# Entry of a feed-forward network: ScalarE's steps put one product behind VectorE's, the chain of operands reordered, weight sums formed ahead of the low parts

## The chip, the cores and the metric

One Trainium2 chip, one core. The time is device microseconds (us) of one execution of the whole program. The kernel before takes 2473.96 us, the median of 3 runs (2471.93 to 2474.3).

## What is computed

One inference step of a one-layer streaming encoder over 544 tokens (512 prompt frames and 32 frames of a running stream), model width 2048, feed-forward width 5632, all in float32. Cut to what the change touches:

```python
mix, s_new, lat_new, kr_new = token_mixer(h, ...)      # ends with  ... @ w_out
h = layer_norm(ALPHA * h + mix, ln1_g, ln1_b)
ff, conv_new = conv_ffn(h, ...)

def conv_ffn(x, conv_buf, w_up, w_gate, conv_w, conv_b, w_down):
    u = x @ w_up
    ext = jnp.concatenate([conv_buf, u], axis=1)
    a = conv_b + sum(ext[:, j:j + T] * conv_w[j] for j in range(CONV_W))
    h = jax.nn.silu(a) * (x @ w_gate)
    return h @ w_down, ext[:, -(CONV_W - 1):]
```

## The kernel before, in words

Activations lie transposed: features on the 128 partitions, tokens along the free axis, in two token halves of 272 (`j` = 0 and 1). Every float32 product is made of three fp32r products, high by high, high by low and low by high. So each operand x is split: `high` (ScalarE, ACT) writes the rounded x, `low` (VectorE, DVE) writes x minus the rounded x. Weights are split in the same way: 512 KB of raw weights land in a `raw` slot, ACT writes `wh` (`rounded`, L962, or `split_w`, L104), DVE writes `wl` (L963, L105). Three `wh` and three `wl` buffers go round.

**The entry.** The layer norm's input z stands in `za` (blocks 0 to 7, feature half 1) and `zb` (blocks 8 to 15, feature half 2). The output projection finishes token half 0 first. Its statistics (sums over partitions by TensorE, L816; means and scales spread back by TensorE, L821) are taken while TensorE (PE) does the last three column groups of token half 1, twelve steps of 24 matmuls (`step`, list `TASKS`). During these, z of token half 0 is normalised in groups of four blocks, `G0` and `G1`: `centred` (DVE, L1119) subtracts the mean, `scaled` (DVE, L1122) multiplies, `affine` (ACT, L1127, four activations and, from ACT's own queue, a DMA that saves the result), then `high` (ACT, L1084) and `low` (DVE, L1088). The weights of the next step are split in between (`split_next`).

**The products.** The up and gate projections use Strassen's seven products (Winograd's form) on 2 by 2 blocks: feature half by token half. The operands are "11" and "12" (token half 0), "21" and "22" (token half 1), and the sums s1, s2, s4, s3 built from them (`summed`, L1473). The weights need sums too: `form` (DVE, L955, in place in a raw slot) and then `prep` (split into wh and wl). One entry of the list `items` is one product with one of the two weight matrices, 24 matmuls of 272 columns (L1011). Pairs of blocks 0 and 1 start as plain products of token half 0, which need only "11" and "12"; product 13 of the list is the first that reads "21", products 21 to 28 read s1, s2, s4, s3 in that order, two of each.

**What sets the order.** The order on PE, DVE and ACT is written out by hand (`manual_schedule`): each engine runs its instructions in the order in which the code issues them. `play` goes through `items`; at each it issues the product, then `prep` of the product two ahead, then `form` of the product three ahead. After that it spends what room is left on `need`, a list that makes the operands of token half 1 step by step (`chain`), each step charged 1.3 us of DVE time; `flush` runs steps early where the next product reads an operand that isn't done. Each step of `chain` names DVE and ACT instructions together. The loads of raw weights are issued by SyncE (SP) as slots come free (`pump`).

The statistics of token half 1 are taken between the first two products of the feed-forward network: `items[0].multiply()`, then `finish(6, ...)` adds the last column group into z and into the sums, then PE's sums of `stats`, then `items[1].multiply()`.

Of the kernel before, what the change touches and what calls it, by code (L numbers as in the profile page):

```python
# [57 lines left out]
def tile_encoder_step(ctx, tc, xp, xs, w_in, w_kr, w_q_b, w_kv_b, w_out, w_up, w_gate, w_down, w_down2,  # L58
# [87 lines left out]
    def pair_half(ps, j):  # L146
        n = H_[j].stop - H_[j].start
        return [ps[:, 512 * t:512 * t + n] for t in range(2)]

    def run(*gens):  # L150
        for g in gens:
            for _ in g:
                pass
# [636 lines left out]
    def acc_tile():  # L790
        seq[0] += 1
        if seq[0] % 2:
            return main_tile()
        return psA.tile([P, 1024], F32, name="acc", tag="acc")

    class Norm:
# [97 lines left out]
        def scale(self, z, e1, e2):  # L894
            z = z[:, self.cols]
            e1.tensor_tensor(out=z, in0=z, in1=self.mub, op=ALU.subtract)
            e2.tensor_tensor(out=z, in0=z, in1=self.rsb, op=ALU.mult)
            return z
# [34 lines left out]
    free, pending, fills, need, gated, retired = [], [], [], [], set(), set()  # L933
# [7 lines left out]
    def pump():  # L941
        while pending and free:
            g, key, src, n = pending.pop(0)
            p, tag = free.pop(0)
            t = p.tile([P, n * P], F32, name=tag, tag=tag)
            dma(t, src)
            g.raw[key] = Raw((p, tag), t)
# [132 lines left out]

    apx = ctx.enter_context(ExitStack())

    def high(name, src, ks):
        A.activation(x1_op[name][ks.start // GK][:, 0], src, AF.Copy)  # L1084

    def low(name, src, ks):
        t = x1_op[name][ks.start // GK]
        V.tensor_tensor(out=t[:, 1], in0=src, in1=t[:, 0].bitcast(F32), op=ALU.subtract)  # L1088

# [25 lines left out]
    def block(b, ks, j):  # L1115
        return (za, zb)[b][:, ks, H_[j]]

    def centred(b, ks, j):
        V.tensor_tensor(out=block(b, ks, j), in0=block(b, ks, j), in1=wide(nrm[j].mub), op=ALU.subtract)  # L1119

    def scaled(b, ks, j):
        V.tensor_tensor(out=block(b, ks, j), in0=block(b, ks, j), in1=wide(nrm[j].rsb), op=ALU.mult)  # L1122

    def affine(b, ks, j):
        for k in range(ks.start, ks.stop):
            zk = zt[b * HK + k][:, H_[j]]
            A.activation(zk, zk, AF.Identity, bias=col(C_LN1_B + b * HK + k), scale=col(C_LN1_G + b * HK + k))  # L1127
        A.dma_start(x1_dr[b][:, ks, H_[j]], block(b, ks, j))

    for t in range(2):  # L1130
        for j in range(2):
            z = zt[t][:, H_[j]]
# [180 lines left out]
    def chunk_of(p):  # L1313
        for g, n in enumerate(CHUNKS):
            if p < n:
                return g, p
            p -= n

    def flush(names):
        while need and any(n not in done for n in names):  # L1320
            need.pop(0)()
            late_need[0] -= 1.3

    done = {"11", "12"}

    def play(items, n0, hooks):

        for n in range(n0, len(items)):
            it = items[n]
            room = it.time  # L1330
            if n and items[n - 1].sink:
                room -= items[n - 1].sink()
            flush((it.name,))
            it.multiply()
            if n + 2 < len(items) and not hasattr(items[n + 2], "w"):
                room -= items[n + 2].prep()
            if n + 3 < len(items):
                pump()
                room -= items[n + 3].form()
            for f in hooks.get(n, ()):  # L1340
                f()
            if need and started:
                late_need[0] += room
                while need and late_need[0] > 0.6:
                    need.pop(0)()
                    late_need[0] -= 1.3
            else:
                drain(room)
            pump()
        items[-1].sink()  # L1350

    late_need, started = [0.0], set()

    with tc.manual_schedule():

# [31 lines left out]
        G0, G1 = GROUPS  # L1387
# [5 lines left out]
        def first_split():  # L1393
# [7 lines left out]
        first_w = []  # L1401
        x11, x12 = (lambda ks, b=b: block(b, ks, 0) for b in range(2))
        halves = [pair_half(acc_tile(), 1) for _ in range(3)]
        TASKS = [
            [lambda: next(stats0), lambda: next(stats0), lambda: [shifted(k, 1) for k in (14, 15, 10)]],
            [lambda: next(stats0), lambda: run(stats0), split_next, lambda: [shifted(k, 1) for k in (11, 12, 13)]],
            [split_next, lambda: centred(0, G0, 0), lambda: scaled(0, G0, 0)],
            [split_next, lambda: centred(0, G1, 0), lambda: affine(0, G0, 0), lambda: scaled(0, G1, 0)],
            [split_next, lambda: finish(7, halves[0]), lambda: affine(0, G1, 0)],
            [split_next, lambda: centred(1, G0, 0), lambda: high("11", x11(G0), G0), lambda: scaled(1, G0, 0)],  # L1410
            [split_next, lambda: high("11", x11(G1), G1), lambda: low("11", x11(G0), G0)],
            [split_next, lambda: affine(1, G0, 0), lambda: low("11", x11(G1), G1)],
            [split_next, lambda: finish(5, halves[1])],
            [first_split],
            [lambda: centred(1, G1, 0), lambda: scaled(1, G1, 0), lambda: affine(1, G1, 0)],
            [lambda: high("12", x12(G0), G0), lambda: high("12", x12(G1), G1)],
        ]
        for n, tasks in enumerate(TASKS):
            step(halves[n // 4], ws7[n] if n < 4 else ws[n - 4], 1, n % 4)
# [4 lines left out]
        items = p0.plain(0, e0)  # L1424
# [14 lines left out]
        finish(6, halves[2])  # L1439
        st_ps = main_tile()  # L1440
        stats = nrm[1].stats(ps=st_ps)
        next(stats)
        next(stats)
        low("12", x12(G0), G0)
        items[1].multiply()
        for it, t in zip(items[2:], sr):
            it.w = rounded(t, HK)
        next(stats)
        run(stats)
        low("12", x12(G1), G1)  # L1450
        st_stack.close()
        ff = ctx.enter_context(pool("ff"))
        ea = ff.tile([P, 4, 546], F32, name="ea", tag="ea")
# [18 lines left out]
        def summed(out, a, b, ks, f):  # L1472
            V.tensor_tensor(out=out[:, ks], in0=a[:, ks], in1=b[:, ks], op=f)  # L1473
# [9 lines left out]
        def open_late():  # L1483
# [3 lines left out]
            add_slots(lt, "rawl", 2)  # L1487

        ADD, SUB = ALU.add, ALU.subtract
        chain = [  # L1490
            [lambda: centred(0, G0, 1)],
            [lambda: scaled(0, G0, 1)],
            [lambda: affine(0, G0, 1), lambda: centred(0, G1, 1)],
            [lambda: scaled(0, G1, 1)],
            [lambda: high("21", a21[:, G0], G0), lambda: affine(0, G1, 1), lambda: centred(1, G0, 1)],
            [lambda: low("21", a21[:, G0], G0)],
            [lambda: scaled(1, G0, 1), lambda: high("21", a21[:, G1], G1)],
            [lambda: affine(1, G0, 1), lambda: centred(1, G1, 1)],
            [lambda: low("21", a21[:, G1], G1), lambda: done.add("21")],
            [lambda: scaled(1, G1, 1), lambda: high("22", a22[:, G0], G0), lambda: affine(1, G1, 1)],  # L1500
            [lambda: low("22", a22[:, G0], G0), lambda: high("22", a22[:, G1], G1)],
            [lambda: summed(a22, a21, a22, G0, ADD)],
            [lambda: low("22", a22[:, G1], G1), lambda: done.add("22"), lambda: high("s1", a22[:, G0], G0)],
            [lambda: summed(a22, a21, a22, G1, ADD)],
            [lambda: low("s1", a22[:, G0], G0), lambda: high("s1", a22[:, G1], G1)],
            [lambda: summed(a22, a22, a11, G0, SUB)],
            [lambda: low("s1", a22[:, G1], G1), lambda: done.add("s1"), lambda: high("s2", a22[:, G0], G0)],
            [lambda: summed(a22, a22, a11, G1, SUB)],
            [lambda: low("s2", a22[:, G0], G0), lambda: high("s2", a22[:, G1], G1)],
            [lambda: summed(a12, a12, a22, G0, SUB), close_wo],  # L1510
            [lambda: low("s2", a22[:, G1], G1), lambda: done.add("s2"), lambda: high("s4", a12[:, G0], G0)],
            [lambda: summed(a12, a12, a22, G1, SUB)],
            [lambda: low("s4", a12[:, G0], G0), lambda: high("s4", a12[:, G1], G1)],
            [lambda: summed(a21, a11, a21, G0, SUB)],
            [lambda: low("s4", a12[:, G1], G1), lambda: done.add("s4"), close_zb, lambda: high("s3", a21[:, G0], G0)],
            [lambda: summed(a21, a11, a21, G1, SUB)],
            [lambda: low("s3", a21[:, G0], G0), lambda: high("s3", a21[:, G1], G1)],
            [lambda: low("s3", a21[:, G1], G1), lambda: done.add("s3"), open_late],
        ]
        need += [lambda fs=fs: [f() for f in fs] for fs in chain]  # L1520


        ysq = [None] * 4
# [44 lines left out]
        class Whole:  # L1568

            n, name = 8, "11"  # L1570
# [28 lines left out]
        NU = len(items)  # L1599
# [11 lines left out]
        def at(n, f):  # L1611
            hooks.setdefault(n, []).append(f)
# [13 lines left out]
        def split_group(g, i):  # L1626
            for b, name in enumerate(("11", "12")):
                t = home[name].tile([P, 2, 2, T], R, name=f"hid{name}", tag=f"op{name}{i}")
                for f in range(2):
                    split_hid(FD + 4 * g + 2 * b + f, staged[g][:, 2 * b + f], t[:, f, 0], t[:, f, 1])  # L1630

        at(2, lambda: started.add(1))
        at(16, late12)
        for i, name in enumerate(ORDER):
# [378 lines left out]
```

## Time and profile before

| | us |
|---|---|
| median of 3 runs | 2473.96 |
| the profiled execution's own time | 2472.49 |
| its span in the profile | 2470.7 |
| PE busy in the span | 2400.2 (97%) |
| DVE busy | 1661.2 (67%) |
| ACT busy | 981.3 (40%) |
| mean granted clock of TensorE, as a share of full | 0.988 |

The profile is of one execution. A busy PE is one with matmuls in flight. The granted clock of TensorE is 1.00 (2.4 GHz) or 0.50 (1.2 GHz); values between are means over a stretch that holds both. In the timeline the bracket at the end of a row says how long the engine had stood idle before it and which instruction ended that.

### The profile page before, as it was taken

To read this page: it belongs to the slowest core of one execution; us is meant where nothing else is said; L and a number is where in the kernel's file an instruction comes from. 1 tells how busy PE (TensorE), PEld (TensorE's weight loads), DVE (VectorE), ACT (ScalarE), POOL (GpSimd) and SP (SyncE) were. 2 spreads that over 40 slices of the span, in tenths; PEclk is the share of its full clock that TensorE was granted. 3 is DMA by queue.
4 is the path that set the end of the run, shared out by engine and by line. 5 is a ranking of instruction groups with operands and counts; after the bars stand their busy time and mean duration, and the time that the engine had idled before them with its cause. 6 is when DMAs were issued, how large, how long until landed. Compare 5 with 4: busy or idle time off the path is not lost.

```text
span 2470.7 us, 44476 instructions
## 1 busy us (share of the span) xinstructions
PE 2400.2 (97%) x18758; PEld 2350.2 (95%) x18758; DVE 1661.2 (67%) x2241; ACT 981.3 (40%) x1475; POOL 181.0 (7%) x212
## 2 busy tenths in 40 slices
PE   7999999999999998989999999999999999999996
PEld 6997799999999998889999999999999999999996
DVE  7444443443435546778888888888777888888566
ACT  4244322222223234545555555555444433333233
POOL 4000011111111110000000000000000100000024
PEclk9999999999999999899999999999999999999998
DMA  7231132222225334534535343443433875632312
GB/s 232 88 94 54 57 108 76 77 77 77 77 76 179 116 117 129 177 111 140 180 113 173 128 156 145 138 162 123 155 107 126 303 303 171 223 136 89 126 56 73
DMA packets 123848, 324.29 MB, mean 131 GB/s; under 512 B 11008, under 2 KB 57856, under 8 KB 119040
## 3 DMA queue, kind: packets, MB, share of 16 engines
q1 hardware_dynamic: 114384, 277.99, 34.3%
q0 software_dynamic: 5040, 39.00, 4.0%
q10 hardware_dynamic: 4224, 4.46, 0.5%
q8 instruction: 147, 2.41, 0.4%
q14 instruction: 53, 0.43, 0.1%
HBM read 266.09 MB, written 53.92 MB: 130 GB/s over the span
## 4 chain that ended last, share of the span: by engine, by line
PE 50%; DVE 4%; ACT 1%; issue 1%; ACTq 0%; DVEq 0%
PE main L1011 18%; PE acc L1011 14%; PE main L1039 8%; PE acc L1039 6%; PE acc L116 3%; PE main L116 2%; DVE wl L963 1%; DVE raw L955 1%; ACT wh L962 1%; DVE n_s L867 0%; DVE y L1821 0%; DVE ea L1253 0%; DVE rawl L955 0%; DVE y L1786 0%; DVE y L1882 0%
## 5 line engine op out<-in xcount | busy, mean ns | idle before, releaser
L963 DVE TENSOR_TENSOR wl<-raw,wh 128x1024 fp32r<-128x1024 f32 x340 | 415.5, 1224 | 193.7 <-ACT wh L962 191.6
L962 ACT ACTIVATE wh<-raw 128x1024 fp32r<-128x1024 f32 x340 | 359.5, 1058 | 433.6 <-DVE raw L955 313.6
L116 PE MATMUL main<-aH,wh 128*128 128x272 f32 (+2 forms) x1536 | 348.9, 296 | 0.5 <-ACT x L262 0.5
L116 PE MATMUL main<-aL,wh 128*128 128x272 f32 (+2 forms) x1536 | 337.8, 289 | 3.7 <-POOL aL L264 3.7
L116 PE MATMUL main<-aH,wl 128*128 128x272 f32 (+2 forms) x1536 | 338.2, 290 | 0.0
L105 DVE TENSOR_TENSOR wl<-raw,wh 128x1024 fp32r<-128x1024 f32 (+2 forms) x128 | 149.7, 1171 | 244.0 <-ACT wh L104 242.7
L104 ACT ACTIVATE wh<-raw 128x1024 fp32r<-128x1024 f32 (+2 forms) x128 | 126.5, 991 | 373.0 <-PE main L116 290.9
L1011 PE MATMUL main<-op,wh 128*128 128x272 f32 x1408 | 268.2, 290 | 2.7 <-ACT wh L962 2.7
L1011 PE MATMUL acc<-ops,wh 128*128 128x272 f32 x1344 | 256.7, 289 | 8.1 <-DVE ops L1088 8.1
L1011 PE MATMUL main<-ops,wh 128*128 128x272 f32 x1344 | 254.5, 288 | 0.5 <-ACT wh L962 0.5
L116 PEld LDWEIGHTS main<-aL,wh 128*128 128x128 f32 x1536 | 250.3, 190 | 4.4 <-POOL aL L264 4.4
L116 PEld LDWEIGHTS main<-aH,wh 128*128 128x128 f32 x1536 | 249.0, 190 | 4.1 <-issue 1.6
L116 PEld LDWEIGHTS main<-aH,wl 128*128 128x128 f32 x1536 | 249.4, 190 | 0.0
L1011 PEld LDWEIGHTS main<-op,wh 128*128 128x128 f32 x1408 | 223.2, 190 | 3.1 <-ACT wh L962 3.1
L1011 PEld LDWEIGHTS acc<-ops,wh 128*128 128x128 f32 x1344 | 213.1, 190 | 8.3 <-DVE ops L1088 8.3
L1011 PEld LDWEIGHTS main<-ops,wh 128*128 128x128 f32 x1344 | 211.1, 188 | 0.7 <-ACT wh L962 0.7
L1011 PE MATMUL main<-op,wl 128*128 128x272 f32 x704 | 204.5, 291 | 1.2 <-DVE wl L963 1.2
L1011 PE MATMUL main<-ops,wl 128*128 128x272 f32 x672 | 194.6, 290 | 2.5 <-DVE wl L963 2.4
L1011 PE MATMUL acc<-ops,wl 128*128 128x272 f32 x672 | 195.3, 291 | 0.8 <-DVE wl L963 0.8
L1011 PE MATMUL acc<-op,wh 128*128 128x272 f32 x832 | 157.6, 288 | 2.1 <-DVE eg L1231 1.5
L962 ACT ACTIVATE wh<-rawl 128x1024 fp32r<-128x1024 f32 x93 | 98.6, 1060 | 129.9 <-DVE rawl L955 75.9
L955 DVE TENSOR_TENSOR raw<-raw,raw 128x1024 f32<-128x1024 f32 x114 | 139.1, 1220 | 0.8
(385 smaller groups left out, 4880.3 us busy)
## 6 DMA issues: line engine op xcount, KB each, us to landing
raw<-in_w_in SPq DMA_DIRECT2D x76, 512.0 KB, 3.6
raw<-in_w_up SPq DMA_DIRECT2D x72, 512.0 KB, 6.3
raw<-in_w_gate SPq DMA_DIRECT2D x72, 512.0 KB, 5.2
raw<-in_w_down SPq DMA_DIRECT2D x71, 512.0 KB, 3.9
raw<-in_w_out SPq DMA_DIRECT2D x40, 512.0 KB, 3.6
opd<-ohl SPq DMA_DIRECT2D x16, 1088.0 KB, 5.6
ops<-opd POOLq DMA_DIRECT2D x16, 1088.0 KB, 9.3
opd<-ohl SPq DMA_DIRECT2D x16, 816.0 KB, 8.7
```

The lines of the kernel that those rows point to most:

```text
L104: A.activation(dst(hv), src(rv), AF.Copy)
L105: V.tensor_tensor(out=dst(lv), in0=src(rv), in1=dst(hv).bitcast(F32), op=ALU.subtract)
L116: PE.matmul(ps, ww[:, wcols[0]:wcols[1]], aa[:, hs[j]], start=first and i == 0, stop=last and i == 2, skip_group_check=True)
L955: V.tensor_tensor(out=out, in0=a, in1=b, op=ALU.subtract)
L962: A.activation(wh, src, AF.Copy)
L963: V.tensor_tensor(out=wl, in0=src, in1=wh.bitcast(F32), op=ALU.subtract)
L1011: PE.matmul(ps, ww[:, k * P:(k + 1) * P], aa, start=self.first and k == 0 and i == 0, stop=k == n - 1 and i == 2, skip_group_check=True)
L1039: PE.matmul(banks[:, 512 * u:512 * u + NI], ww[:, (u * n + k) * P:(u * n + k + 1) * P], aa, start=self.first and k == 0 and i == 0, stop=k ...
```

## The change

Four things are changed, all in the order in which instructions are issued; no instruction is added or left out on PE, DVE and ACT but those of waiting.

1. In `TASKS` the steps that normalise token half 0 are put together (`normalised`: `affine` and at once `high`) and stand elsewhere among the splits; `first_split` stands behind the last of them.
2. `items[1].multiply()` stands ahead of PE's sums of token half 1, and the rest of the statistics is issued after the product with index 2.
3. `chain` becomes a list of pairs: what DVE does, and what ACT does with its result. The second part is put off (`after`, `follow`) until the next product and the preparation behind it have been issued, or until a step needs it.
4. In `play`, for the feed-forward products, `form` of the product three ahead is issued before `prep` of the product two ahead.

```diff
+        def normalised(b, ks):
+            return [lambda: affine(b, ks, 0), lambda: high(("11", "12")[b], block(b, ks, 0), ks)]
+
         TASKS = [
...
-            [split_next, lambda: centred(0, G1, 0), lambda: affine(0, G0, 0), lambda: scaled(0, G1, 0)],
-            [split_next, lambda: finish(7, halves[0]), lambda: affine(0, G1, 0)],
-            [split_next, lambda: centred(1, G0, 0), lambda: high("11", x11(G0), G0), lambda: scaled(1, G0, 0)],
-            [split_next, lambda: high("11", x11(G1), G1), lambda: low("11", x11(G0), G0)],
-            [split_next, lambda: affine(1, G0, 0), lambda: low("11", x11(G1), G1)],
-            [split_next, lambda: finish(5, halves[1])],
+            [split_next, *normalised(0, G0), lambda: centred(0, G1, 0), lambda: scaled(0, G1, 0)],
+            [split_next, lambda: finish(7, halves[0]), *normalised(0, G1), lambda: low("11", x11(G0), G0)],
+            [split_next, lambda: centred(1, G0, 0), lambda: scaled(1, G0, 0)],
+            [split_next, *normalised(1, G0), lambda: low("11", x11(G1), G1), lambda: centred(1, G1, 0)],
+            [split_next, lambda: scaled(1, G1, 0)],
+            [split_next, lambda: finish(5, halves[1]), *normalised(1, G1), lambda: low("12", x12(G0), G0)],
             [first_split],
-            [lambda: centred(1, G1, 0), lambda: scaled(1, G1, 0), lambda: affine(1, G1, 0)],
-            [lambda: high("12", x12(G0), G0), lambda: high("12", x12(G1), G1)],
+            [lambda: low("12", x12(G1), G1)],
+            [],
...
         stats = nrm[1].stats(ps=st_ps)
+        items[1].multiply()
         next(stats)
         next(stats)
-        low("12", x12(G0), G0)
-        items[1].multiply()
         for it, t in zip(items[2:], sr):
             it.w = rounded(t, HK)
-        next(stats)
-        run(stats)
-        low("12", x12(G1), G1)
...
+        at(2, lambda: next(stats))
+        at(2, lambda: run(stats))
         at(2, lambda: started.add(1))
...
+    def follow():
+        for f in after:
+            f()
+        after.clear()
+
+    def advance():
+        fs, behind = need.pop(0)
+        if any(isinstance(f, tuple) and f[0] not in rounded_ops for f in fs):
+            follow()
+        for f in fs:
+            (f[1] if isinstance(f, tuple) else f)()
+        after.extend(behind)
+        late_need[0] -= 1.3
...
             it.multiply()
-            if n + 2 < len(items) and not hasattr(items[n + 2], "w"):
-                room -= items[n + 2].prep()
-            if n + 3 < len(items):
-                pump()
-                room -= items[n + 3].form()
+            for ahead in ((3, 2) if n + 3 < NU else (2, 3)):
+                if n + ahead < len(items):
+                    pump()
+                    room -= items[n + ahead].prep() if ahead == 2 else items[n + ahead].form()
+            follow()
...
+        def scale(n, ks):
+            b, z = blocks[n]
+            return [lambda: scaled(b, ks, 1)], [lambda: affine(b, ks, 1), lambda: high(n, z[:, ks], ks)]
```

**How the order moves, place one: ACT at the end of the output projection.** `wh` is a split of the projection's weights, `za` and `zb` are z, `op_8047` and `op_8048` the operand "11" (G0, G1), `op_8052` the operand "12" (G0), `n_e` the squares for the statistics. Before:

```order
L1127 ACTIVATE za<-za,par 128x272 x4
L1128 DMA x1d_8037<-za 128x4x272
L104 ACTIVATE wh<-raw 128x1024
L863 ACTIVATE n_e<-zb 128x272 x2
L1127 ACTIVATE za<-za,par 128x272 x4
L1128 DMA x1d_8037<-za 128x4x272
L104 ACTIVATE wh<-raw 128x1024
L1084 ACTIVATE op_8047<-za 128x1088
L104 ACTIVATE wh<-raw 128x1024
L1084 ACTIVATE op_8048<-za 128x1088
L104 ACTIVATE wh<-raw 128x1024
L1127 ACTIVATE zb<-zb,par 128x272 x4
```

Now:

```order
L1131 ACTIVATE za<-za,par 128x272 x4
L1132 DMA x1d_8037<-za 128x4x272
L1087 ACTIVATE op_8047<-za 128x1088
L104 ACTIVATE wh<-raw 128x1024
L863 ACTIVATE n_e<-zb 128x272 x2
L1131 ACTIVATE za<-za,par 128x272 x4
L1132 DMA x1d_8037<-za 128x4x272
L1087 ACTIVATE op_8048<-za 128x1088
L104 ACTIVATE wh<-raw 128x1024 x2
L1131 ACTIVATE zb<-zb,par 128x272 x4
L1132 DMA x1d_8038<-zb 128x4x272
L1087 ACTIVATE op_8052<-zb 128x1088
```

Each rounding of an operand now stands ahead of a weight split that stood ahead of it.

**Place two: ACT around product 13.** `raw_10174` (now `raw_10176`) are the weights of product 13, the first that reads "21"; `op_10065` and `op_10066` (now `op_10048`) are the operand "22", `ea` is a copy of a finished product. Before:

```order
L962 ACTIVATE wh<-raw_10106 128x1024
L962 ACTIVATE wh<-raw_10137 128x1024
L1084 ACTIVATE op_10065<-zb 128x1088
L1127 ACTIVATE zb<-zb,par 128x272 x4
L1128 DMA x1d_8038<-zb 128x4x272
L1084 ACTIVATE op_10066<-zb 128x1088
L1218 ACTIVATE ea<-acc 128x544
L962 ACTIVATE wh<-raw_10174 128x1024
```

Now:

```order
L962 ACTIVATE wh<-raw_10107 128x1024
L962 ACTIVATE wh<-raw_10139 128x1024
L1222 ACTIVATE ea<-acc 128x544
L962 ACTIVATE wh<-raw_10176 128x1024
L1131 ACTIVATE zb<-zb,par 128x272 x4
L1132 DMA x1d_8038<-zb 128x4x272
L1087 ACTIVATE op_10048<-zb 128x1088
L962 ACTIVATE wh<-raw_10213 128x1024
```

The weights of product 13 are now rounded ahead of the affine step and the rounding of "22", where they stood behind both.

**Place three: DVE between the operands s4 and s3.** L1473 (now L1490) makes s3, L1088 (now L1092) makes low parts, `ops_10593` (now `ops_10591`) is s4 (G1), `ops_10784` is s3 (G0), L955 forms a weight sum in a raw slot, L963 makes the low part of weights. Before:

```order
L1473 TENSOR_TENSOR za<-za 128x4x272
L1088 TENSOR_TENSOR ops_10593<-zb,ops_10593 128x1088
L963 TENSOR_TENSOR wl<-raw_10622,wh 128x1024
L955 TENSOR_TENSOR raw_10516<-raw_10581,raw_10516 128x1024
L963 TENSOR_TENSOR wl<-raw_10516,wh 128x1024
L955 TENSOR_TENSOR raw_10549<-raw_10622,raw_10549 128x1024
L963 TENSOR_TENSOR wl<-raw_10549,wh 128x1024
L955 TENSOR_TENSOR raw_10816<-raw_10816,raw_10451 128x1024
L1473 TENSOR_TENSOR za<-za 128x4x272
L1227 TENSOR_TENSOR eg<-ea,main 128x2x272
L1088 TENSOR_TENSOR ops_10784<-za,ops_10784 128x1088
```

Now:

```order
L1490 TENSOR_TENSOR za<-za 128x4x272
L1092 TENSOR_TENSOR ops_10591<-zb,ops_10591 128x1088
L955 TENSOR_TENSOR raw_10519<-raw_10592,raw_10519 128x1024
L963 TENSOR_TENSOR wl<-raw_10625,wh 128x1024
L955 TENSOR_TENSOR raw_10551<-raw_10625,raw_10551 128x1024
L963 TENSOR_TENSOR wl<-raw_10519,wh 128x1024
L955 TENSOR_TENSOR raw_10811<-raw_10811,raw_10453 128x1024
L963 TENSOR_TENSOR wl<-raw_10551,wh 128x1024
L1490 TENSOR_TENSOR za<-za 128x4x272
L1231 TENSOR_TENSOR eg<-ea,main 128x2x272
L1092 TENSOR_TENSOR ops_10784<-za,ops_10784 128x1088
```

A sum and the low part that is made from it had nothing between them; now another low part stands between.

## Rows read from the trace of the kernel before

**Rows 1.** Busy time by stretch, core 0: us, PE, PEld, DVE, ACT, POOL, granted clock, DMA

```profile
986.00:997.00 11.00, 8.36 (x42) 8.33 (x42) 6.74 (x11) 3.61 (x5) 1.83 (x1) 0.56 0.64 245
1033.40:1043.00 9.60, 9.09 (x49) 8.77 (x50) 8.63 (x8) 5.09 (x6) 0.00 (x0) 0.65 0.52 165
1043.00:1055.00 12.00, 12.00 (x98) 12.00 (x97) 11.96 (x11) 7.33 (x9) 0.00 (x0) 1.00 0.52 170
```

**Rows 2.** Timeline of PE, statistics of token half 1: start us, us, engine, line, operation

```profile
981.36 0.29 PE L1011 MATMUL main<-op,sl 128*128 128x272 f32 x1
988.64 2.72 PE L816 MATMUL main<-ones,n_s 128*128 128x1 f32 x12 [6.99 <-DVE n_s L858]
...
996.33 0.74 PE L821 MATMUL main<-ident,nt_dm 128*128 128x128 f32 x6
...
998.30 0.50 PE L1011 MATMUL acc<-op,wh 128*128 128x272 f32 x2
```

**Rows 3.** Timeline of PE, the same sums for token half 0

```profile
939.76 1.40 PE L816 MATMUL main<-ones,n_s 128*128 128x1 f32 x12
```

**Rows 4.** Timeline of ACT, end of the output projection

```profile
956.34 1.06 ACT L104 ACTIVATE wh<-raw 128x1024 fp32r<-128x1024 f32 x1 [0.52 <-ACT za L1127]
...
960.67 2.12 ACT L1127 ACTIVATE za<-za,par 128x272 f32<-128x272 f32 x4
...
963.56 1.06 ACT L104 ACTIVATE wh<-raw 128x1024 fp32r<-128x1024 f32 x1 [0.78 <-ACT za L1127]
964.53 1.09 ACT L1084 ACTIVATE op<-za 128x1088 fp32r<-128x1088 f32 x1
```

**Rows 5.** Timeline of PE, end of the output projection

```profile
964.67 0.40 PE L116 MATMUL acc<-aH,wh 128*128 128x272 f32 x1 [0.32 <-ACT wh L104]
...
965.93 0.40 PE L116 MATMUL acc<-aH,wl 128*128 128x272 f32 x1 [0.74 <-DVE wl L105]
```

**Rows 6.** Timeline of PE around products 13 and 14

```profile
1030.50 0.29 PE L1011 MATMUL main<-op,wl 128*128 128x272 f32 x1
1033.47 0.82 PE L1011 MATMUL main<-op,wh 128*128 128x272 f32 x2 [2.68 <-ACT wh L962]
...
1042.99 0.41 PE L1011 MATMUL acc<-op,wh 128*128 128x272 f32 x2
```

**Rows 7.** Timeline of ACT ahead of product 13

```profile
1028.28 2.13 ACT L1127 ACTIVATE zb<-zb,par 128x272 f32<-128x272 f32 x4 [2.89 <-DVE zb L1122]
...
1032.37 1.99 ACT L962 ACTIVATE wh<-raw 128x1024 fp32r<-128x1024 f32 x2
```

**Rows 8.** Timeline of DVE ahead of product 13, then between s4 and s3

```profile
1028.16 1.28 DVE L1088 TENSOR_TENSOR op<-zb,op 128x1088 fp32r<-128x1088 f32 x1
...
1076.73 1.23 DVE L963 TENSOR_TENSOR wl<-raw,wh 128x1024 fp32r<-128x1024 f32 x1 [2.19 <-ACT wh L962]
...
1080.22 1.23 DVE L963 TENSOR_TENSOR wl<-raw,wh 128x1024 fp32r<-128x1024 f32 x1 [1.13 <-ACT wh L962]
...
1083.78 1.23 DVE L963 TENSOR_TENSOR wl<-raw,wh 128x1024 fp32r<-128x1024 f32 x1 [1.20 <-ACT wh L962]
...
1087.89 2.48 DVE L1088 TENSOR_TENSOR ops<-za,ops 128x1088 fp32r<-128x1088 f32 x2
```

**Rows 9.** Timeline of PE: products 25, 27 (its third matmul), 29 and 73

```profile
1073.07 0.41 PE L1011 MATMUL main<-ops,wh 128*128 128x272 f32 x2
...
1089.23 0.59 PE L1011 MATMUL acc<-ops,wh 128*128 128x272 f32 x1 [8.08 <-DVE ops L1088]
...
1099.35 0.48 PE L1011 MATMUL acc<-op,wh 128*128 128x272 f32 x2 [1.52 <-DVE eg L1231]
...
1237.75 0.41 PE L1011 MATMUL main<-op,wh 128*128 128x272 f32 x2
```

**Rows 10.** Waits of DVE from 1100 to 1250: us in total, times, longest

```profile
DVE wl L963 <- ACT wh L962: 23.7, 20, 3.3
```

**Rows 11.** The page's costliest groups: the weight sums; count, busy, mean ns, idle before

```profile
L955 DVE TENSOR_TENSOR raw<-raw,raw 128x1024 f32<-128x1024 f32 x114 | 139.1, 1220 | 0.8
```

More of the change, by code (lines that the diff above doesn't have):

```diff
@@ L1081, in tile_encoder_step @@
     apx = ctx.enter_context(ExitStack())
+    rounded_ops = set()
     def high(name, src, ks):
+        rounded_ops.add((name, ks.start))
         A.activation(x1_op[name][ks.start // GK][:, 0], src, AF.Copy)
     def low(name, src, ks):
+        assert (name, ks.start) in rounded_ops
         t = x1_op[name][ks.start // GK]
@@ L1317, in chunk_of @@
             p -= n
+    def follow():
[10 more added lines that the diff above has]
+        late_need[0] -= 1.3
     def flush(names):
         while need and any(n not in done for n in names):
-            need.pop(0)()
-            late_need[0] -= 1.3
+            follow()
+            advance()
     done = {"11", "12"}
@@ L1334, in play @@
             it.multiply()
-            if n + 2 < len(items) and not hasattr(items[n + 2], "w"):
-                room -= items[n + 2].prep()
-            if n + 3 < len(items):
-                pump()
-                room -= items[n + 3].form()
+            for ahead in ((3, 2) if n + 3 < NU else (2, 3)):
+                if n + ahead < len(items):
+                    pump()
+                    room -= items[n + ahead].prep() if ahead == 2 else items[n + ahead].form()
+            follow()
             for f in hooks.get(n, ()):
@@ L1344, in play @@
                 while need and late_need[0] > 0.6:
-                    need.pop(0)()
-                    late_need[0] -= 1.3
+                    advance()
             else:
@@ L1350, in play @@
         items[-1].sink()
-    late_need, started = [0.0], set()
+    late_need, started, after = [0.0], set(), []
     with tc.manual_schedule():
@@ L1489, in tile_encoder_step @@
         ADD, SUB = ALU.add, ALU.subtract
[L1490 to L1518, printed above, removed]
@@ new lines, in tile_encoder_step, with centre, lower, total @@
+        blocks = {"21": (0, a21), "22": (1, a22)}
+        def centre(n, ks):
+            return [lambda: centred(blocks[n][0], ks, 1)], []
+        def scale(n, ks):
+            b, z = blocks[n]
+            return [lambda: scaled(b, ks, 1)], [lambda: affine(b, ks, 1), lambda: high(n, z[:, ks], ks)]
+        def lower(n, z, ks, *then):
+            return [((n, ks.start), lambda: low(n, z[:, ks], ks)), *([lambda: done.add(n)] if ks is G1 else []), *then], []
+        def total(n, out, a, b, ks, f, *then):
+            return [lambda: summed(out, a, b, ks, f), *then], [lambda: high(n, out[:, ks], ks)]
@@ new lines, in tile_encoder_step @@
+        need += [
+            centre("21", G0), scale("21", G0), centre("21", G1), scale("21", G1), centre("22", G0), scale("22", G0),
+            lower("21", a21, G0), centre("22", G1), lower("21", a21, G1), scale("22", G1), lower("22", a22, G0),
+            total("s1", a22, a21, a22, G0, ADD), lower("22", a22, G1), total("s1", a22, a21, a22, G1, ADD),
+            lower("s1", a22, G0), total("s2", a22, a22, a11, G0, SUB), lower("s1", a22, G1),
+            total("s2", a22, a22, a11, G1, SUB), lower("s2", a22, G0), total("s4", a12, a12, a22, G0, SUB, close_wo),
+            lower("s2", a22, G1), total("s4", a12, a12, a22, G1, SUB), lower("s4", a12, G0),
+            ([lambda: summed(a21, a11, a21, G0, SUB)], []),
+            (lower("s4", a12, G1, close_zb)[0], [lambda: high("s3", a21[:, G0], G0)]),
+            total("s3", a21, a11, a21, G1, SUB), lower("s3", a21, G0), lower("s3", a21, G1, open_late),
@@ L1519, in tile_encoder_step @@
         ]
-        need += [lambda fs=fs: [f() for f in fs] for fs in chain]
         ysq = [None] * 4
```

## The prediction

> **What bounds the kernel now.** I read the page first, for the engine that is busy throughout (TensorE, PE), then the waits and the timeline of PE for the places where it stood still, then the timelines of ACT and DVE at those places, and last the busy time by stretch for the granted clock. PE works without a pause in most of the span, so only what shortens its pauses counts, and they lie close together between 960 and 1240 us. The reader is to see four. (1) After the first feed-forward product PE stands 6.99 us for the sums of token half 1, and the statistics and the next product then run at half clock [rows 1, 2]. (2) Product 13 waits 2.68 us for its weights on ACT and then runs at half clock [rows 1, 6]. (3) Product 27 stands 8.08 us for the low part of s3 [rows 9]. (4) From product 29 to 73 small waits add up. A product at full clock takes 3.01 us: products 15 to 24 went from 1042.99 to 1073.07, 30.08 us for ten [rows 6, 9].
>
> **The change part by part.** Each term compares PE's progress with before.
>
> **A, end of the output projection: a loss.** The change puts `high` of "11" ahead of weight splits on ACT. One `high` takes 1.09 us and, in a row of instructions, about 1.0 of ACT's time [rows 4]. The first moves the split of 956.34, the additions to z behind it, their squares and so the affine step of 960.67 back by 1.0; the second stands right behind that step. So the split that began at 963.56 begins at 965.6, and PE, which waited 0.32 for it [rows 4, 5], waits 2.0 more; its low part is again 0.74 behind. The split after the next stands behind the affine step of `zb`, which needs DVE's `scaled`: DVE can do the late split's low part (1.23, until 967.9), then `centred` and `scaled` until 970.4; affine 2.13, the DMA issue 0.5 and `high` 1.0 bring the split to 974.0 and its end to 975.1. PE gets there two steps of 3.0 after 967.4, with the 0.4 that it waits before as well: at 974. That is 0.8 and, for the low part, 0.7. Then `first_split`: it now follows the squares of group 5 (PE ends that group at 979, squares until 980.6), affine, issue and `high` until 984.1, so its first half ends at 985.2. PE is done with the projection at 982.1: a wait of 3.1, and 0.9 for the low part. Sum 2.0 + 1.5 + 4.0 = **+7.5**. x1's DMAs move with the affine steps, and the eight loads that `first_split` sets free start some 8 us later on SP; they are read by products 3 to 10, the last of which comes 25 us later, and I cost them at nothing. If they were late, ACT's first splits of the products would be.
>
> **The clock.** The wait of 2.68 before product 13 put PE at half clock: from 1030.63 to 1042.99 two products took 12.36 where 6.02 were due, and 2.68 and about 0.8 of waits leave 2.9 [rows 6]. The 1.52 before product 29 put it nowhere: of 44 products behind it, none runs at half clock. The wait of 3.1 in A lies by the first of these, so I take **+2.9**; bounds 0 and twice 2.9.
>
> **B, the statistics: a gain.** Before, PE went from 981.49 to 998.30 for one product, the sums and the spreading: 16.81 us [rows 2]. Now two products stand ahead of the sums, and finish(6)'s additions and squares fit under them: DVE needed 0.4 for each of six, ACT's squares come behind the two `first_split` activations at about 990, and PE asks for the sums only at 992 or later. What remains is the product (3.01), the sums at full clock (1.40 [rows 3] against 2.72) and the spreading, 1.97 [rows 2]. **-10.4**. The cover is the two products; without it up to 7.0 would be back.
>
> **C, product 13: a gain.** ACT rounded its weights at 1032.37, behind an affine step that had waited 2.89 for DVE's `scaled`, and behind `high` [rows 7]. Now the split stands ahead of both. Next to be late is its low part on DVE: it follows the low part that began at 1028.16 directly, so it runs from 1029.4 to 1030.6, and PE wants it at 1030.9 [rows 6, 8]. So the whole 12.36 - 6.02 = 6.3 goes but for what DVE takes back: it was busy 11.96 of 12.00 us in the next stretch [rows 1], and a split's low part behind two other steps will be some tenths late, two or three times. I take **-5.3**, bounds -6.3 and -2.
>
> **D, products 25 to 28: a gain.** From 1073.07 to 1099.35 four products took 26.28 where 12.03 were due [rows 9]. Before s3's low part at 1087.89 DVE made three weight sums with their low parts and stood 2.19, 1.13 and 1.20 us still, each time for ACT's `wh` of the sum that it had just made [rows 8]. With another low part between, ACT rounds while DVE works: 4.5 us go from the chain that ends PE's wait, and the waits of s4's weights ahead of it with them. The wait of 8.08 stays near 4.5, long enough for the clock to fall as before. **-5.0**, bounds 0 and -6.
>
> **E, products 29 to 72: a gain.** 44 products took 138.40 where 132.4 were due [rows 9]. DVE stood 23.7 us in 20 waits for `wh` there [rows 10]: the same pattern, sum, rounding, low part. With DVE 20 us freer, I take **-5.5**, bounds -2 and -6. Later PE has next to no waits to lose.
>
> Sum: 7.5 + 2.9 - 10.4 - 5.3 - 5.0 - 5.5 = **-15.8 us**. The profiled execution took 2472.49, 1.5 below the median of the three runs; 2473.96 - 15.8 is 2458.2, and I say **2458**.
>
> **Rivals.**
> *The clock falls more than once in A.* The wait at 964.6 (2.3 us, with 0.74 close behind) lies between the 1.52 that did nothing and the 2.68 that did. Then 2.9 or 5.8 more: 2461 to 2464. For: product 13's row; against: PE does matmuls between the two waits. The Trainium skill, "TensorE: Matmul & The Clock Gate", section "HAM oscillation — how this bites in real kernels", says that a kernel which stands still again and again pays for the fall each time. By that rule A's waits would cost up to three falls; the trace agrees as far as it goes, with three falls behind waits of 2.68, 6.99 and 8.08.
> *DVE is the bound from product 13 on.* Its 11.96 of 12.00 us say so, the pauses of [rows 8] speak against it. Then C loses 3 to 4, D all 5: 2466 to 2468.
> *Sums wait for their loads.* On the other side. `form` now stands ahead of the low part that PE needs next, so a raw block that lands late holds up PE, where before it held up a product further off. DVE stood 0.8 us in all ahead of 114 such sums [rows 11], so before none was late. It decides if loads land more than about a sum (1.22 us) later against their use than now: one such wait in each of the 20 pairs would cost over 1.1 x 20 = 22, and the time would be 2480.
>
> **How the numbers follow.** A measurement of this kernel tells about 0.2% from no change, 4.9 us: 2469.0 to 2478.9. The forecast has 0.62, the clock rival 0.18, the DVE rival 0.12 (a third of it beyond 2469 with a second fall), the loads 0.05, the rest 0.03. Faster: 0.62 + 0.18 + 0.07 = 0.87, taken as 0.86; same 0.08; slower 0.06. The range goes from no fall in A and the far bounds of C, D and E, -15.8 - 2.9 - 2 = 2453, to the DVE rival with a fall, 2469.
>
> **What would show it.** Right: PE waits of 2 to 3 us behind ACT's `wh` near 965 and 982; none for the sums; product 13 without a wait over 1 us; the wait for s3's low part near 4.5; DVE's pauses before `wl` about 20 us fewer from product 29 to 73. Wrong: weight sums with idle time before them, or a wait for the sums or of product 13 that stays.

## The result and the profile after

The changed kernel takes 2452.27 us, the median of 4 runs (2452.0 to 2454.08), the kernel before 2472.97 in the same comparison; the ratio is 0.9918, interval 0.9900 to 0.9935. It is faster, as forecast, but by 20.7 us where 15.8 were forecast, and 0.7 below the range. The head of the page of the changed kernel:

```profile
span 2450.5 us, 44552 instructions
PE 2393.8 (98%) x18758; PEld 2346.8 (96%) x18758; DVE 1668.6 (68%) x2241; ACT 977.1 (40%) x1475; POOL 180.0 (7%) x212
```

The span is 20.2 shorter. Where it came from is read off the starts of the products on PE (the first of 24 matmuls, each product counted through), in the same execution as the spans:

| start of | before | after | gained so far | this stretch | forecast |
|---|---|---|---|---|---|
| product 1 | 978.46 | 984.96 | +6.5 | | |
| product 4 | 1001.40 | 1001.12 | -0.3 | -0.3 | 0.0 (A, clock and B: 7.5 + 2.9 - 10.4) |
| product 15 | 1042.99 | 1036.47 | -6.5 | -6.2 | -5.3 (C) |
| product 29 | 1099.35 | 1087.12 | -12.2 | -5.7 | -5.0 (D) |
| product 73 | 1237.75 | 1219.49 | -18.3 | -6.0 | -5.5 (E) |
| end of span | 2470.7 | 2450.5 | -20.2 | -1.9 | 0 |

The timeline of PE of the changed kernel (start, duration, operation, in brackets the wait ahead of it):

```profile
966.23 0.39 PE L116 MATMUL acc<-aH,wh 128*128 128x272 f32 x1 [1.91 <-ACT wh L104]
...
967.49 0.40 PE L116 MATMUL acc<-aH,wl 128*128 128x272 f32 x1 [0.74 <-DVE wl L105]
...
976.01 0.39 PE L116 MATMUL acc<-aH,wl 128*128 128x272 f32 x1 [0.71 <-DVE wl L105]
...
984.96 0.51 PE L1011 MATMUL main<-op,sh 128*128 128x272 f32 x2 [2.94 <-ACT sh L1414]
986.22 0.59 PE L1011 MATMUL main<-op,sl 128*128 128x272 f32 x1 [0.75 <-DVE sl L1415]
...
994.79 1.39 PE L816 MATMUL main<-ones,n_s 128*128 128x1 f32 x12
996.05 0.50 PE L1011 MATMUL acc<-op,wh 128*128 128x272 f32 x2
...
1030.02 0.41 PE L1011 MATMUL main<-op,wh 128*128 128x272 f32 x2
...
1033.61 0.39 PE L1011 MATMUL main<-op,wl 128*128 128x272 f32 x1 [0.17 <-DVE wl L963]
...
1078.00 0.59 PE L1011 MATMUL acc<-ops,wh 128*128 128x272 f32 x1 [4.43 <-DVE ops L1092]
...
1087.12 0.49 PE L1011 MATMUL acc<-op,wh 128*128 128x272 f32 x2 [1.64 <-DVE eg L1235]
...
1219.49 0.41 PE L1011 MATMUL main<-op,wh 128*128 128x272 f32 x2
```

Of the waits of [rows 5] the 0.32 has grown to 1.91, the 0.74 behind it is as before, and new ones of 2.94 and 0.75 stand at product 1. The 6.99 for the sums [rows 2], the 2.68 of product 13 [rows 6] and 3.65 of the 8.08 of product 27 [rows 9] are gone (the wait of product 27 stands at its second matmul, the first that reads a low part of s3). Product 14, the row of 1033.61, waits a little for its low part. From 1087.12 to 1219.49 no wait is left: 44 products in 132.37. The busy time by stretch (us, PE, PEld, DVE, ACT, POOL, granted clock, DMA) shows where the clock stood at half:

```profile
968.00:972.00 4.00, 4.00 (x22) 4.00 (x21) 3.96 (x4) 1.94 (x4) 0.00 (x0) 0.57 0.46 131
985.00:992.50 7.50, 6.75 (x30) 6.54 (x31) 6.89 (x10) 2.67 (x4) 0.00 (x0) 0.54 0.65 217
1077.50:1081.00 3.50, 3.00 (x13) 3.00 (x14) 3.50 (x4) 1.62 (x4) 0.00 (x0) 0.51 0.58 191
```

The clock fell once behind the two waits at 966, once behind the 2.94, and once for product 27, there for a shorter time than before. The timeline of DVE ahead of product 27:

```profile
1067.58 1.22 DVE L955 TENSOR_TENSOR raw<-raw,raw 128x1024 f32<-128x1024 f32 x1
1068.71 1.22 DVE L963 TENSOR_TENSOR wl<-raw,wh 128x1024 fp32r<-128x1024 f32 x1
1069.85 1.22 DVE L955 TENSOR_TENSOR raw<-raw,raw 128x1024 f32<-128x1024 f32 x1
1070.99 1.22 DVE L963 TENSOR_TENSOR wl<-raw,wh 128x1024 fp32r<-128x1024 f32 x1
1072.55 1.22 DVE L955 TENSOR_TENSOR raw<-raw,raw 128x1024 f32<-128x1024 f32 x1 [0.35 <-DMA raw<-in_w_up]
```

The three pauses for `wh` of [rows 8] are gone. From product 29 to 73 DVE waits for `wh` (total, times, longest):

```profile
DVE wl L963 <- ACT wh L962: 10.6, 18, 2.0
```

In the kernel before, between the same two products:

```profile
DVE wl L963 <- ACT wh L962: 21.3, 18, 3.3
```

### The profile page after: what moved, and what is told of

Its sections match the earlier page's. It is cut to its first block, busy times and chain, and to the rows that moved or that the text cites. A ratio compares the mean times of both kernels' runs of the same rounds, so it can differ in the third digit from the quotient of the medians.

```text
span 2450.5 us, 44552 instructions
## 1 busy us (share of the span) xinstructions
PE 2393.8 (98%) x18758; PEld 2346.8 (96%) x18758; DVE 1668.6 (68%) x2241; ACT 977.1 (40%) x1475; POOL 180.0 (7%) x212
## 4 chain that ended last, share of the span: by engine, by line
PE 78%; DVE 4%; ACT 1%; issue 1%; DMA 0%; ACTq 0%; DVEq 0%
PE main L1011 20%; PE main L116 19%; PE acc L1011 16%; PE main L1039 8%; PE acc L116 6%; PE acc L1039 6%; PE s L664 1%; DVE wl L963 1%; DVE n_s L867 0%; PE sw L725 0%; PE sw L697 0%; ACT zb L1131 0%; PE sw L727 0%; PE s L703 0%; DVE y L1835 0%
## 5 line engine op out<-in xcount | busy, mean ns | idle before, releaser
L963 DVE TENSOR_TENSOR wl<-raw,wh 128x1024 fp32r<-128x1024 f32 x340 | 415.5, 1222 | 133.5 <-ACT wh L962 132.6
L955 DVE TENSOR_TENSOR raw<-raw,raw 128x1024 f32<-128x1024 f32 x114 | 139.2, 1221 | 1.9 <-DMA raw<-in_w_up 0.3
```

What stands on the lines that cost most here:

```text
L955: V.tensor_tensor(out=out, in0=a, in1=b, op=ALU.subtract)
L963: V.tensor_tensor(out=wl, in0=src, in1=wh.bitcast(F32), op=ALU.subtract)
```

## The experiments

Ten further kernels and the change once more, in three groups (u1 to u4; a34 to y2; y3 to after_again), each measured beside the kernel before. Ahead of the change, where the code is the same, the profiled executions differ by up to 3.9 us: the spreading of the scales of token half 0 (L821) begins at 944.19 in u1 and at 948.06 in a4. So beside the times stands the start of a product counted from that instruction, less the same in the kernel before. All are read from the one profiled execution.

| run | median us | ratio, interval | product 4 | 15 | 29 | 73 | end of span |
|---|---|---|---|---|---|---|---|
| the change | 2452.27 | 0.9900 to 0.9935 | -0.2 | -6.5 | -12.2 | -18.2 | -20.2 |
| u1_tasks_as_before | 2452.06 | 0.9901 to 0.9928 | -1.3 | -7.5 | -13.0 | -19.0 | -20.9 |
| u2_stats_as_before | 2452.27 | 0.9903 to 0.9930 | -0.4 | -6.7 | -12.7 | -18.7 | -20.6 |
| u3_chain_as_before | 2458.80 | 0.9929 to 0.9954 | -0.4 | -0.2 | -6.6 | -12.7 | -14.6 |
| u4_prep_first | 2467.33 | 0.9964 to 0.9985 | -0.5 | -6.7 | -7.1 | -7.1 | -6.9 |
| a34_parts_3_and_4 | 2454.28 | 0.9909 to 0.9934 | -0.5 | -6.8 | -11.7 | -17.8 | -19.6 |
| a4_part_4_alone | 2459.36 | 0.9926 to 0.9951 | -0.3 | -0.4 | -6.9 | -12.9 | -14.8 |
| y1_tail_reordered | 2445.44 | 0.9871 to 0.9901 | -10.0 | -16.2 | -21.4 | -27.4 | -29.3 |
| y2_chain_two_steps_ahead | 2441.10 | 0.9856 to 0.9883 | -9.5 | -13.4 | -23.9 | -30.0 | -31.8 |
| y3_chain_ahead_from_13 | 2442.55 | 0.9863 to 0.9893 | -9.0 | -15.2 | -22.6 | -28.6 | -30.5 |
| y4_chain_ahead_from_7 | 2439.81 | 0.9851 to 0.9884 | -9.4 | -13.2 | -24.6 | -30.6 | -32.5 |
| after_again | 2453.71 | 0.9908 to 0.9938 | -0.7 | -7.0 | -11.7 | -17.7 | -19.6 |

The kernel before took 2472.35, 2473.72 and 2472.60 in the three groups.

### One part undone

**Part 1.** `TASKS` as before, and

```diff
         next(stats)
         next(stats)
+        low("12", x12(G0), G0)
+        low("12", x12(G1), G1)
         for it, t in zip(items[2:], sr):
```

> The change without its part 1 (TASKS and first_split as before; the two low parts of "12" behind the sums). Theory, terms add: the waits at 966 and 982 and the two clock falls behind them go, product 1 starts at 978.5 again; the sums of half 1 are asked for at 984.5 and wait about 4 us for squares that stand behind two roundings on ACT; product 4 starts at about 999 instead of 1001.1. Time 2450 (2449 to 2451). Rival, parts 1 and 2 need each other: the late low parts of "12" and the wait for the sums eat it all, 2452 to 2455.

The time, 2452.06, is that of the rival; the trace shows both theories at work. PE of this kernel:

```profile
987.43 2.72 PE L816 MATMUL main<-ones,n_s 128*128 128x1 f32 x12 [3.96 <-DVE n_s L858]
...
991.43 0.60 PE L1011 MATMUL acc<-op,wl 128*128 128x272 f32 x1 [0.62 <-DVE wl L963]
```

The tail's waits are gone, and the wait for the sums is 4.0, as worked out, with the clock at half behind it. By product 4 it is ahead of the change by 1.1 us, not by 2. Beside the other three parts, part 1 is worth nothing.

**Part 2.** The statistics between the first two products, the spreading ahead of product 3, as before:

```diff
-        items[1].multiply()
         next(stats)
         next(stats)
+        items[1].multiply()
...
+        next(stats)
+        run(stats)
...
-        at(2, lambda: next(stats))
-        at(2, lambda: run(stats))
```

> The change without its part 2 (sums of half 1 behind one product again, spreading ahead of product 3). Theory of the prediction, that the second product is the cover of the sums: a wait for the sums of 3 to 7 us comes back, 2456 to 2459. Rival, that part 1 alone brings the squares early enough: finish(6) ends at 991.1 on DVE, and PE, later by 6.5 and at half clock, ends product 1 at 991.4, so no wait, 2452 to 2453.

The rival: 2452.27, and PE asks for the sums once with no wait, behind one product:

```profile
984.45 0.82 PE L1011 MATMUL main<-op,sh 128*128 128x272 f32 x2 [2.94 <-ACT sh L1414]
...
990.86 1.55 PE L816 MATMUL main<-ones,n_s 128*128 128x1 f32 x12
```

The second product is not what covers the sums: with part 1 PE comes 6 us later anyway, and the roundings that stood ahead of the squares on ACT are done. As far as this wait goes, parts 1 and 2 do the same thing twice; part 2 without part 1 (u1) leaves 4.0 of it.

**Part 3.** `need` filled from the `chain` of before, nothing put off:

```diff
+        need += [(fs, []) for fs in chain]
```

> The change without its part 3 (the chain's order of before, ACT's step issued with DVE's). Theory: the wait of product 13 for its weights and its fall of the clock come back, 6.3 us, and nothing else: 2458 to 2459.5, with a wait for ACT's wh of about 2.7 at product 13. Rival, that the sums ahead of the low parts already free ACT there: 2452 to 2454.

The theory: 2458.80, 6.5 more, all of it by product 15, with the old wait back:

```profile
1035.43 0.82 PE L1011 MATMUL main<-op,wh 128*128 128x272 f32 x2 [2.69 <-ACT wh L962]
```

This undoes two things together, the putting off of ACT's steps and the new order of the chain; which of them brings the gain is not shown.

**Part 4.**

```diff
-            for ahead in ((3, 2) if n + 3 < NU else (2, 3)):
+            for ahead in (2, 3):
```

> The change without its part 4 (low parts ahead of weight sums again). Theory: all gains behind product 15 go, 5.7 to product 29, 6.0 to product 73, 2 behind it: 2464 to 2467, and DVE waits for wh some 20 us more from product 29 to 73. Rival, that part 3 alone leaves DVE enough room: 2452 to 2457.

The theory, 0.3 over its range: 2467.33, 15.1 more by the medians, 13.3 by the traces (-6.9 against -20.2). Product 27 waits 7.59 again, the small waits behind product 48 are back, and DVE stands for `wh`; PE, then two pauses of DVE ahead of s3's low part, then the waits of DVE from 1100 to 1250 here (the change: 11.5 us, 21 times):

```profile
1084.67 0.59 PE L1011 MATMUL acc<-ops,wh 128*128 128x272 f32 x1 [7.59 <-DVE ops L1092]
```

```profile
1075.66 1.23 DVE L963 TENSOR_TENSOR wl<-raw,wh 128x1024 fp32r<-128x1024 f32 x1 [1.13 <-ACT wh L962]
...
1079.22 1.23 DVE L963 TENSOR_TENSOR wl<-raw,wh 128x1024 fp32r<-128x1024 f32 x1 [1.21 <-ACT wh L962]
```

```profile
DVE wl L963 <- ACT wh L962: 24.9, 21, 3.3
```

Both pumps of `play` stay in this kernel, so that the loads are issued at one more place in each turn is not what brings the gain.

### Parts added to the kernel before

**Parts 3 and 4 alone** (both undoings of parts 1 and 2 together).

> The kernel before with parts 3 and 4 of the change alone (TASKS and statistics as before). Theory, that parts 1 and 2 are worth nothing together (product 4 started 0.3 us earlier than before in the changed kernel): the wait of 7 us for the sums and its fall of the clock are back, the waits at 966 and 982 are gone, product 4 starts as before, product 15 6.3 earlier, product 73 18 earlier; 2452.5 (2451.5 to 2453.5). Rival, that the statistics' order is a gain of its own, 10.4 less what the tail costs: 2455 to 2460.

2454.28, between the two ranges, 0.8 over the theory's, with an interval that is nearly that of the change. Product 4 starts about as before, as the theory says. Parts 1 and 2 together are worth 2.0 us against the change's first median, 0.6 against its second (2453.71, after_again) and 0.6 by the traces: nothing that these runs tell from zero. The old wait of 6.98 for the sums stands in its profile.

**Part 4 alone** (only the line of part 4 above, the other way; the helpers of part 3 are there, but nothing is put off).

> The kernel before with part 4 alone (weight sums ahead of low parts). Theory, terms add: nothing up to product 15, where the wait of 2.7 and its half clock stay, then 5 to product 29, 6 to product 73, 2 behind it: 2459 (2457.5 to 2460). Rival, that part 4 needs the chain of part 3, without which ACT is late: 2463 to 2468.

The theory: 2459.36. Nothing to product 15, then all that D, E and the last stretch gave. It needs no help from part 3.

### What the tail and the chain leave

Product 4 starts no earlier in the change than before, and product 27 still waits 4.43. Four kernels go after these two losses, with parts 2 to 4 kept.

**Another order of the tail**, in place of part 1 (lines of `TASKS` of before, changed):

```diff
-            [split_next, lambda: finish(7, halves[0]), lambda: affine(0, G1, 0)],
-            [split_next, lambda: centred(1, G0, 0), lambda: high("11", x11(G0), G0), lambda: scaled(1, G0, 0)],
+            [split_next, lambda: finish(7, halves[0]), lambda: affine(0, G1, 0), lambda: centred(1, G0, 0), lambda: scaled(1, G0, 0)],
+            [split_next, lambda: high("11", x11(G0), G0), lambda: centred(1, G1, 0), lambda: scaled(1, G1, 0)],
...
-            [split_next, lambda: finish(5, halves[1])],
+            [split_next, lambda: affine(1, G1, 0), lambda: finish(5, halves[1])],
             [first_split],
-            [lambda: centred(1, G1, 0), lambda: scaled(1, G1, 0), lambda: affine(1, G1, 0)],
-            [lambda: high("12", x12(G0), G0), lambda: high("12", x12(G1), G1)],
+            [lambda: high("12", x12(G0), G0), lambda: high("12", x12(G1), G1)],
+            [lambda: low("12", x12(G0), G0), lambda: low("12", x12(G1), G1)],
```

> Parts 2 to 4, and in place of part 1 another order of the tail: centring and scaling of "12" in DVE's idle time at 961, its affine steps in ACT's idle time at 972, so that nothing stands ahead of the last squares. Theory: no waits above 0.8 in the projection's tail, sums at once behind product 2 at 984.5, no fall of the clock ahead of product 4, which starts at 990 to 992 instead of 1001; the chain starts as much earlier, so all of it stays: 2442 (2441 to 2446). Rival, that the transfers set the pace there (371 to 413 GB/s from 984 to 992): product 5 waits for its weights, 2447 to 2451. Second rival, that DVE, busy 9.6 to 9.96 of each 10 us from 1040 to 1080, gives it back ahead of product 27: 2448 to 2452.

The theory: 2445.44, in its range. The sums follow product 2 with no wait, product 5 has no wait for its weights, which speaks against the first rival, product 4 gains 10, and nearly all of it lasts to the end, with 3.99 of wait left at product 27:

```profile
986.09 1.39 PE L816 MATMUL main<-ones,n_s 128*128 128x1 f32 x12
...
988.12 0.39 PE L1011 MATMUL acc<-op,wl 128*128 128x272 f32 x1 [0.28 <-DVE wl L963]
```

**The chain ahead of its pace**, from the start, from product 13, from product 7 (each on top of y1; the second with index 12, the third with 6):

```diff
-    late_need, started, after = [0.0], set(), []
+    late_need, started, after = [2.6], set(), []
```

```diff
+        at(12, lambda: late_need.__setitem__(0, late_need[0] + 2.6))
```

> As y1_tail_reordered, and the chain of operands has 2.6 us of DVE time in hand from the start, so that two of its steps come earlier. Theory, that product 27 waits because the chain is paced too late while DVE has 2 to 3 idle us in each 10 from 1000 to 1030: the wait of 4.4 shrinks by about 2.6 and its fall of the clock with it, 2 to 5 below y1. Rival, that the early steps stand ahead of low parts of weights: waits of products 9 to 13 grow instead, the same as y1 or 1 to 3 above it.

> As y1_tail_reordered, and the chain gets the 2.6 us in hand only behind the product with index 12, that is product 13. Theory, that only the steps of s4 and s3 have to come earlier: products 9 to 15 start as in y1 (14.7 us earlier than before at product 15), the wait for s3's low part is near 1.4 as in y2, 2 to 4 below y2, so 2437 to 2439. Rival, that DVE, busy for 15.0 of 15 us from 1030 to 1045 in y1, makes the low parts of weights late there instead: waits of 0.3 to 1.2 at products 15 to 24, the same as y2 (2440 to 2442).

> As y1_tail_reordered, and the 2.6 us in hand behind the product with index 6, product 7, past the first steps. By the theory that any early step costs what it displaces: between y2 and y1_tail_reordered's loss, 2440 to 2443; by the theory that only the waits of products 9 and 10 in y2 (0.94 and 0.74) came from the first steps: 2438 to 2440.

All three medians are below that of y1. y2 was measured beside it, 4.3 lower, its highest run (2443.11) just below the lowest of y1 (2443.22). y3 and y4 are of another group, and their intervals overlap with that of y1; that they are faster rests on their traces too (-30.5 and -32.5 against -29.3, one execution each). With y2 both halves of the forecast came: product 27 waits 1.42 with no fall of the clock, and new waits of 0.94 and 0.74 stand at product 9. With y3, 2442.55, the rival had the place and the time within 0.6, but not the wait: at product 16 PE stands 2.13, for ACT's `wh` and not for DVE, and 0.74 for the low part. y4 has the lowest median, 2439.81. That is in the range of the second theory and 0.2 below that of the first, but its trace shows what the first says: four steps of the chain in a row stand ahead of the low part that product 10 waits 2.67 for, and by product 15 it has lost as much against y1 as y2 (3.0 and 2.8 us). PE of y2, of y4, then of y3:

```profile
1010.13 0.52 PE L1011 MATMUL acc<-op,wh 128*128 128x272 f32 x2 [0.94 <-ACT wh L962]
...
1070.77 0.39 PE L1011 MATMUL acc<-ops,wh 128*128 128x272 f32 x1 [1.42 <-DVE ops L1092]
```

```profile
1013.44 0.60 PE L1011 MATMUL acc<-op,wl 128*128 128x272 f32 x1 [2.67 <-DVE wl L963]
...
1068.41 0.39 PE L1011 MATMUL acc<-ops,wh 128*128 128x272 f32 x1 [0.55 <-DVE ops L1092]
```

```profile
1033.02 0.52 PE L1011 MATMUL acc<-op,wh 128*128 128x272 f32 x2 [2.13 <-ACT wh L962]
```

**The change once more**, in the group of y3 and y4.

> The changed kernel itself, unaltered, beside the other two: 2452.3 (2451 to 2454), the same as in the first comparison. If it comes out elsewhere by more than 1.5, the differences of under 2 us between runs of different calls mean nothing.

2453.71. In this group y4 is 13.9 us below it, and their intervals do not touch. All four runs of y4 lie below all four of y3. y2, of another group, is told apart from neither.

## Why the prediction was right and wrong

**A, a loss: the place right, the size too large.** Waits of 1.91 and 2.94 stand where 2.3 and 3.1 were forecast. The split after the next was to be 0.8 late and was not: it ended 0.4 earlier than I had it, and PE, which the first fall of the clock had put back, came to it at 974.9 instead of 974. With the low parts the tail's waits grew by 1.59 + 0.32 + 3.69 = 5.6, not 7.5.

**The clock: more than the term.** I took one fall at 2.9. There were two, 968.3 to 971.8 and 985.4 to 992.2 at half clock; half of these 10.3 us is an estimate of their cost, 5.1. The rival that names two falls was right on the mechanism and wrong on the time, since A's waits were 1.9 smaller and the other terms larger than in the sum it starts from. The rule of the Trainium skill that stood beside that rival ("TensorE: Matmul & The Clock Gate", section "HAM oscillation — how this bites in real kernels"), that a kernel pays again at each long wait, agrees with these two stretches.

**B: the size near, the reason wrong.** A, clock and B together gave -0.3 where 0.0 was forecast. That is luck: A was 1.9 too large and the clock 2.2 too small, and what is left for B is -0.3 - 5.6 - 5.1 = -11.0, where -10.4 was said. And the sentence "The cover is the two products; without it up to 7.0 would be back" fell with u2: nothing came back. And u1 shows that the two products alone leave 4.0 of the 7.0.

**C, D, E: the mechanisms right, each near its far bound.** The stretch of C gave 6.2. Of the 6.3 that could go, 5.9 went: products 12 to 14 took 15.37 us before and take 9.46. Product 14's low part was late, as I had held back for, but once and not two or three times: it takes 3.45, 0.4 too long. The rest is products 9 and 10, 0.4 shorter, for which the sum had no term. D was 5.7, bound 6; the wait of product 27 was 4.43 where "near 4.5" was said, the waits of product 26 (0.50 and 0.74 before) went with it, as was said too, and what came on top is a shorter stretch at half clock. That last part can be chance: after_again has the same wait and the longer stretch, and its D is 4.7 (-11.7 against -7.0). One reading in D was wrong: the first of the three pauses of [rows 8], 2.19, was not for a sum just made, since the step ahead of it is the low part of s4. In u4, where the sums stand as before, the 1.13 and the 1.21 are back and the 2.19 is not. E was 6.0, bound 6. u3 puts C down to part 3 alone, u4 and a4 put D and E down to part 4 alone. One sign of E was wrong: DVE's pauses for `wh` fell by 10.7 us, not by 20. That was enough, since all of PE's waits went.

**The step that failed: "Later PE has next to no waits to lose."** The sum has nothing for the span behind product 73, and no row stands behind that sentence. PE lost 1.9 us there. Product 79 took 4.04 us before, with a wait of 0.76 for a low part, and takes 3.01 now. And another wait of the kernel before is gone. Both, as they were (the second from the waits of PE from 1960 to 2060):

```profile
1256.96 0.39 PE L1011 MATMUL acc<-ops,wl 128*128 128x272 f32 x1 [0.76 <-DVE wl L963]
```

```profile
PE acc L1039 <- ACT eg L1257: 1.2, 1, 1.2
```

Without part 4 both return (0.77 and 1.3 in u4), and with part 4 alone both are gone (a4). I had followed PE no further than product 73, while the same `play` issues the products behind it. The wait of product 79 is of the pattern of E. The other stands at the fourth product of the down projection, for which part 4 no longer changes the order; how part 4 removes it is not shown.

So of the 4.4 missing by the traces (20.2 against 15.8), 1.9 is this step, 2.2 the discounts in C, D and E, and 0.3 the first stretch. The low end of the range let C, D and E reach their bounds, but no stretch gain that I had priced at nothing: 1.9 us later the time would lie inside. It has a slip as well: from the terms to the bounds are 1.0, 1.0 and 0.5, which is 2.5 and not 2, and the end would be 2452.8. And it counts from 2473.96, the median of 3 runs, where the kernel before took 2472.97 beside the changed one. The gain at the low end, 20.7 us, is the gain that was measured, so that the 0.7 by which the time misses the range is no more than this shift of 1.0.

**The rivals on DVE and on the loads.** DVE was busy 11.99 of 12.00 us from 1043 to 1055, and products 20 and 21 lost 0.7 for it; with the 0.4 of product 14 that is 1.1, where the rival has 8 to 9. Weight sums stood 1.9 us in all (0.8 before [rows 11]):

```profile
L955 DVE TENSOR_TENSOR raw<-raw,raw 128x1024 f32<-128x1024 f32 x114 | 139.2, 1221 | 1.9 <-DMA raw<-in_w_up 0.3
```

## What to carry to other kernels

Where two in-order engines hand work to each other (sum, rounding, low part), put one independent step between each hand-over; this one line gave some 14 of the 20 us. The reordering of the tail gave nothing as it was made here, and 7 to 9 us in another order (y1), with which no wait of the tail grew. Follow such a pattern to the end of the loop that issues it, not to the last wait that is easy to see. And where two edits each remove the same wait, undo them one by one before crediting either.

## What was not expected of the hardware

The stretch at half clock doesn't follow from the wait's length. Before, the clock stood at half for 6.6 us around product 13, with a wait of 2.68; in y4, with one of 2.67, for 3.5. Even the same kernel with the same wait differs: the change shows 1077.5 to 1081.0 at a wait of 4.43, and after_again 7 us at one of 4.44, and product 27 takes 10.1 us there where it takes 9.0 in the change. A difference of 1 us between two kernels at such a place can be this alone. Rows of the kernel before, of y4 and of after_again (the columns as above):

```profile
1033.40:1040.00 6.60, 6.09 (x25) 5.77 (x26) 6.55 (x6) 3.02 (x4) 0.00 (x0) 0.50 0.48 157
```

```profile
1013.00:1016.50 3.50, 3.06 (x14) 3.06 (x15) 3.50 (x4) 2.70 (x5) 0.00 (x0) 0.53 0.58 180
```

```profile
1076.50:1083.50 7.00, 5.99 (x27) 5.99 (x28) 4.43 (x4) 2.69 (x6) 0.00 (x0) 0.51 0.77 282
```

What sets its length stays open.
